# Two gate blocks ahead of the sets, single form loads in the weights' queue, single branch pieces, later gates' operands fetched at once

## The chip, the cores and the metric

The kernel runs on one core of a Trainium2 chip. Its engines each run their own instructions in order: TensorE (PE in the profile) multiplies matrices, VectorE (DVE) and ScalarE (ACT) work on tiles, GpSimd (POOL) and SyncE (SP) mainly start DMAs here. They wait for each other through semaphores. The metric is the device time of one execution in microseconds (us), the median of several runs.

## The reference

One decoder layer on 256 rows of width 2048, in float32:

```python
h = _rmsnorm(x, pre_norm_g)
proj = jnp.einsum('bsd,de->bse', h, w_in)
(q_a, c_kv, k_rope, z_mla, c_in, b_gate, c_gate, z_conv, g_mla, g_conv) = jnp.split(proj, cuts, axis=-1)
...
attn = attn.reshape(b, s, MLA_WIDTH) * jax.nn.silu(z_mla)
y_mla = jnp.einsum('bse,ed->bsd', attn, w_o_mla)
u = c_gate * c_in
...
y_conv = jnp.einsum('bse,ed->bsd', b_gate * conv * jax.nn.silu(z_conv), w_o_conv)
merged = jax.nn.sigmoid(g_mla) * y_mla + jax.nn.sigmoid(g_conv) * y_conv
out = jnp.einsum('bsd,de->bse', merged, w_out)
x = x + _rmsnorm(out, post_norm_g)
```

`attn` is causal latent attention with 16 heads of width 128 (query and key/value projections of rank 512, rotary part of 64), and `conv` a causal convolution of three taps over `u`. Apart from the latent projections, the weights of each path are 2048 by 2048.

## The kernel before

Every float32 product is made of three matmuls: each operand is split into a high part (ACT, `whi`, `shi_*`, line 252) and the rest (DVE, `wlo`, `slo_*`, line 253), and high·high, high·low and low·high are summed in PSUM. All matmuls have line 88 in the profile. Weights come in **units** of 1 MB (128 rows of 2048 values) through `load_raw` (line 164, queue of SP) into three buffers `raw`; a unit is split in two halves into `whi` and `wlo`, five buffers each.

**Heads** (0 to about 604 us, lines 520 to 1029). After the latent projections a loop goes over the 16 heads. In each, `channels(h, i)` makes the conv channels and `gates_turn` the gates z, with attention between them. The results are stored in DRAM as `far_at` and `far_cv`. Sprinkled into the heads 1 to 7 is the generator `make_forms` (lines 829 to 880), three steps a head: it loads the transposed input `xf` in two chunks of two DMAs (line 835), scales it (840), makes sums and differences of its quarters (851), splits each into high and low (856, 858, 860) in a tile `form` with two buffers, and stores it to `far_form` (863, POOL's queue, kept in program order). There are seven forms, of 1 MB each.

**Sets** (about 604 to 966 us). Work stands in a list `seq` of items `[load, split, mm, after]`. The driver (lines 1341 to 1368) issues at item j the loads of up to four later items that have one, then the splits of items up to j + 2, then item j's matmuls, then its `after`. Kinds of items:

- Plain units of `gate_block`, `branch_block` and `merged_block`: one weight unit, 24 matmuls. Four make a block of 512 output columns, and `last` treats the PSUM of the block: a gate block makes the sigmoid of `x @ W` and stores it (`keep`), a branch block multiplies by a gate fetched from DRAM (`again`) and stores, a merged block takes the second branch, multiplies, adds the first, turns the sum (line 330) and stores it to `far_m`.
- `paired(c)` for c = 1, 2, 3, the **sets** `s1` to `s3`: the columns of block c of both gates, computed by a scheme of Strassen's kind with seven products of half size in place of eight. The seven, in order `Q1 V5 V6 V7 V4 V3 Q2`, have two items each of 12 matmuls against a form (`sX`, `sY`, `sZ` in the profile). Their weights `b` (line 1174, SP's queue) lie in six buffers; `V5`, `V6` and `V4` add two weight tiles on DVE (line 1182), and `V5` starts a DMA of POOL that adds another tile in place (line 1186).
- `turned_unit`: loads stored pieces of `far_at` or `far_cv` into a `raw` buffer (line 1081) and splits them into `at_both` or `cv_both` (`split_turned`), with no matmul. `at_both` lies where `x_both`, the input of the gate blocks, lay.

`interleave(s, {...})` puts the listed plain and turned items between the items of the set's seven products. The order before: gate block 0 of the first gate (four units), then `s1` with the second gate's block 0 (`g0`), the pieces of `at_both` and the first branch blocks `p`, then `s2`, `s3`, then the merged blocks `v[2]`, `v[3]`. All seven forms are loaded back from `far_form` by POOL ahead of the list (line 1033).

In `merged_block`, `soon` runs after the second unit and fetches operands; for c = 2 and 3 it fetches for both row halves, and for c = 3 it also multiplies (line 1146) `m` (the first branch) by its gate `q`.

**Out stage** (about 966 us to the end, lines 1370 to 1479). `out_order` lists the 16 units of the last product: the first three K quarters of columns 0 and 1 (six units), their last quarters, then columns 2 and 3. `m_both[3]`, the last quarter of its input, comes from `far_m[3]` through the turned unit `last_m`: `last_m[0]` loads it in the first unit, `last_m[1]` splits it. It is needed from the seventh unit. After three units the tiles of the pool `late` are released, and ACT issues the loads of `gb` and `xr` (lines 1399, 1400) into other tiles there.

Where an instruction is not kept in program order by `tc.keep_in_program_order`, the framework may place it elsewhere in its engine's order.

Of the kernel before, what the change touches and what calls it, by code (L numbers as in the profile page):

```python
# [11 lines left out]
F32 = mybir.dt.float32  # L12
F32R = mybir.dt.float32r
I32 = mybir.dt.int32
AF = mybir.ActivationFunctionType
ALU = mybir.AluOpType
PSUM = bass.MemoryType.PSUM

P = 128
S = 256  # L20
NT = S // P
# [61 lines left out]
def tile_layer(ctx: ExitStack, tc: tile.TileContext, xw, w0, xb, x, pos, pvec, post_g, wc, wz, wcv, wkr, wqk, wqr, wv, cwr, wsq, xf, out):  # L83
    nc = tc.nc
# [16 lines left out]
    dram = ctx.enter_context(tc.tile_pool(name="dram", bufs=1, space=bass.MemoryType.DRAM))  # L101
# [17 lines left out]
    for h in range(H):  # L119
        g, second = divmod(h, HG)  # L120
# [23 lines left out]
    out_order = [(c, k) for c in range(2) for k in range(3)] + [(0, 3), (1, 3)]  # L144
    out_order += [(c, k) for c in (2, 3) for k in range(4)]
    u_out = {ck: add(wsq[4, ck[0], ck[1]]) for ck in out_order}
# [71 lines left out]
    def take(i):  # L218
        ahead(i)
        return pieces(splits.pop(i))  # L220
# [93 lines left out]
    n = 2 * XW // S  # L314
# [207 lines left out]
    for i in range(KD // 2):  # L522
# [3 lines left out]
        w = take(u_qa[i])  # L526
# [3 lines left out]
    for i in range(4):  # L530
        w = take(u_ckv[i])
# [9 lines left out]
    w = splits.pop(u_kr)  # L541
# [153 lines left out]
    def values(h, pt):  # L695
# [24 lines left out]
    far_at, far_cv, far_m = (  # L720
        [dram.tile([P, NT * 512], F32, name=f"far_{n}{g}") for g in range(4)] for n in ("at", "cv", "m")
    )
# [101 lines left out]
    cv_w = bp.tile([P, NT, 512], F32, name="cv_w")  # L824
    KH = KD // 2
    FORMS = ("11", "5", "6", "7", "22", "3", "12")
    far_form = {n: dram.tile([P, KH * 2 * P], F32R, name=f"far_form{n}") for n in FORMS}

    def make_forms():

        kq = KH // 2
        for c in range(2):
            area = at_f[:, 8:, :].rearrange("p (i k) s -> p i k s", i=2)
            for i in range(2):
                nc.sync.dma_start(out=area[:, i], in_=xf[i][:, c * kq * S : (c + 1) * kq * S].rearrange("p (k s) -> p k s", k=kq))
            yield
            for i in range(2):
                for k in range(kq):
                    x = area[:, i, k, :]
                    nc.vector.scalar_tensor_tensor(  # L840
                        x, x, col("pre_g", KH * i + kq * c + k), r_x[:, :], op0=ALU.mult, op1=ALU.mult
                    )
                yield
            a11, a21 = area[:, 0, :, :P], area[:, 0, :, P:]
            a12, a22 = area[:, 1, :, :P], area[:, 1, :, P:]
            u, w, f7, f3 = (
                cv_f[:, 8 + 2 * i : 10 + 2 * i, :].rearrange("p a (b s) -> p (a b) s", b=2) for i in range(4)
            )

            def tt(o, a, b, op):  # L850
                nc.vector.tensor_tensor(o, a, b, op=op)

            def part(n, src, sign=1.0):
                f = early_pool.tile([P, kq, 2, P], F32R, name=f"form{n}_{c}", tag="form", bufs=2)
                hi, lo = f[:, :, 0, :], f[:, :, 1, :]
                nc.scalar.activation(hi, src, AF.Copy, scale=sign)
                if sign == 1.0:
                    nc.vector.tensor_tensor(lo, src, hi.bitcast(F32), op=ALU.subtract)
                else:
                    nc.vector.scalar_tensor_tensor(lo, src, sign, hi.bitcast(F32), op0=ALU.mult, op1=ALU.subtract)  # L860
                w = kq * 2 * P
                return lambda: tc.keep_in_program_order(
                    nc.gpsimd.dma_start(
                        out=far_form[n][:, c * w : (c + 1) * w], in_=f[:, :, :, :].rearrange("p k j c -> p (k j c)")
                    )
                )

            goes = []
            for n, src, sign, s in (
                ("11", a11, 1.0, None), ("22", a22, 1.0, None), ("12", a12, 1.0, None), ("5", u, 1.0, (u, a22, a21, ALU.subtract)),  # L870
                ("6", w, -1.0, (w, u, a11, ALU.add)), ("7", f7, 1.0, (f7, a11, a21, ALU.subtract)),
                ("3", f3, 1.0, (f3, w, a12, ALU.subtract)),
            ):
                if s:
                    tt(*s)
                go = part(n, src, sign)
                yield
                go()
        while True:
            yield  # L880
# [16 lines left out]
    for h in range(H):  # L897
        v, at = divmod(h, HV)
# [56 lines left out]
        if 0 < h < 8:  # L955
            next(form_steps)
        channels(h, 2)
        if 0 < h < 8:
            next(form_steps)
        if 0 < h < 8:  # L960
            next(form_steps)

        steps = [make(*i, *([at == 3] if i[0] == "a" else [])) for i in made[h]]
# [62 lines left out]
    def again(key, t):  # L1026
        tc.keep_in_program_order(nc.gpsimd.dma_start(out=t[:, :], in_=kept[key][:, :]))  # L1027
# [1 line left out]


    form = {n: forms.tile([P, KH, 2, P], F32R, name=f"form_{n}") for n in FORMS}
    for n in FORMS:
        nc.gpsimd.dma_start(out=form[n][:, :, :, :].rearrange("p k j c -> p (k j c)"), in_=far_form[n][:, :])


    seq = []
# [36 lines left out]
    def turned_unit(far, both, first, queue=nc.sync):  # L1073


        box = []

        def load():
            t = wpool.tile([P, UNIT], F32, name=f"turned{len(seq)}_{first}", tag="raw", bufs=3)
            for i, f in enumerate(far):  # L1080
                queue.dma_start(out=t[:, i * 1024 : (i + 1) * 1024], in_=f[:, :])
            box.append(t)

        def split():
            for i in range(len(far)):
                for t in range(NT):
                    o = i * 1024 + t * 512
                    split_turned(box[0][:, o : o + 512], both[first + i], t)

        return [load, split, None, None]  # L1090
# [18 lines left out]
    def branch_block(c, both):  # L1109
# [19 lines left out]

        return block(c, 2, lambda k: both[k // 4][:, k % 4, :], {}, last)  # L1130

    def merged_block(c, both):

        got = []

        def fetch(t):
            g, m = (
                wide(f"v{n}{c}_{t}", "y", 2) if c < 2 else late.tile([P, 512], F32, name=f"v{n}{c}_{t}")
                for n in "gm"
            )  # L1140
            again(("gc", c, t), g)
            again(("y" if c == 3 else "m", c, t), m)
            if c == 3:
                q = late.tile([P, 512], F32, name=f"vq{t}")
                again(("gm", c, t), q)
                nc.vector.tensor_tensor(m[:, :], m[:, :], q[:, :], op=ALU.mult)  # L1146
            got.append((g, m))

        def soon():
            for t in range(1 if c < 2 else NT):  # L1150
                fetch(t)

        def last(pss):
            for t in range(NT):
                if len(got) <= t:
                    fetch(t)
                g, m = got[t]
                nc.vector.tensor_tensor(g[:, :], pss[t][:, :], g[:, :], op=ALU.mult)
                nc.vector.tensor_tensor(m[:, :], m[:, :], g[:, :], op=ALU.add)  # L1159
                go, _ = turned(m[:, :], g[:, :], 4, far_m[c][:, 512 * t : 512 * (t + 1)])  # L1160
                go()

        return block(c, 3, lambda k: both[k // 4][:, k % 4, :], {1: soon}, last)
# [100 lines left out]
    def interleave(s, after):  # L1264

        for name in ("Q1", "V5", "V6", "V7", "V4", "V3", "Q2"):
            seq.extend(s[name])
            seq.extend(after.get(name, []))
# [9 lines left out]
    class Late(list):  # L1278
# [10 lines left out]
    make_identity(nc, ident[:, :])  # L1289
    seq.extend(gate_block(0, 0, "gm", {}))  # L1290
    at_b, cv_b = Late("at"), Late("cv")
    at_u = [turned_unit(far_at[2 * i : 2 * i + 2], at_b, 2 * i) for i in range(2)]
    cv_u = [turned_unit(far_cv[2 * i : 2 * i + 2], cv_b, 2 * i) for i in range(2)]
    g0 = gate_block(0, 1, "gc", {})
    p = [branch_block(c, at_b) for c in range(4)]
    v = [merged_block(c, cv_b) for c in range(4)]
    s1, s2, s3 = (paired(c) for c in (1, 2, 3))
    gate_last, branch_last = s2["Q2"][1][3], p[2][3][3]
    p[2][3][3] = None
    s2["Q2"][1][3] = lambda: (gate_last(), branch_last())  # L1300
    interleave(s1, {
        "Q1": g0[:1], "V5": g0[1:2], "V6": g0[2:3], "V7": g0[3:] + at_u[:1], "V4": at_u[1:] + p[0][:2],
        "V3": p[0][2:], "Q2": p[1][:3],
    })
    interleave(s2, {
        "Q1": p[1][3:], "V5": p[2][:1], "V6": p[2][1:2], "V7": p[2][2:3], "V4": p[2][3:], "Q2": p[3][:1],
    })
    interleave(s3, {
        "Q1": p[3][1:2], "V5": p[3][2:3], "V6": p[3][3:] + cv_u[:1], "V7": cv_u[1:] + v[0][:1], "V4": v[0][1:3],
        "V3": v[0][3:], "Q2": v[1],  # L1310
    })
    m_b = Late("m")
    m_pool, late, lstack = {}, None, ExitStack()
# [65 lines left out]
    def out_products(pss, w, kk):  # L1379
        for t in range(NT):  # L1380
            out_product(pss[t], t, w, kk)

    pss = [[bank(f"out{c}_{t}") for t in range(NT)] for c in range(2)]
    for i, (c, kk) in enumerate(out_order[:3]):
        w = take(u_out[c, kk])
        if i == 0:
            last_m[0]()
        if i == 2:
            last_m[1]()
        out_products(pss[c], w, kk)  # L1390
    lstack.close()
    main.close()
# [65 lines left out]
        normed(t, 1536, 2048, rr)  # L1458
        store(t, 1536, 2048, og[:, t, cs])

    for c, kk in out_order[3:6]:
        out_products(pss[c], take(u_out[c, kk]), kk)
    for c in range(3):
        if c == 2:
            pss.append([bank(f"out{c}_{t}") for t in range(NT)])
# [105 lines left out]
```

## Time and profile before

| what | value |
| --- | --- |
| median of 3 runs | 1075.21 us (1072.54 to 1075.4) |
| the profiled execution | 1075.93 us |
| its span in the trace | 1074.1 us |
| DVE busy | 786.3 us (73%) |
| ACT busy | 577.5 us (54%) |
| POOL busy | 205.4 us (19%) |
| HBM traffic | 239.78 MB read, 28.31 MB written |

The span runs from the first to the last recorded instruction of the profiled execution. A name such as `out<-whi,m_both` gives the tile written and the tiles read. A row of the timeline has its start, its length, the engine, the source line, the operation and shape, the count, and in brackets the idle time ahead of it with the tile or instruction that ended it; `SPq`, `ACTq` and `POOLq` rows are what an engine's queue does by itself, such as starting DMAs. The granted clock is the share of full speed that TensorE's throttle granted.

### The profile page before, as it was taken

The page shows a single profiled execution, that of the slowest core. Times are in us where ns is not written, and L with a number is a line of the kernel's source. Part 1 is how long each engine was busy: PE and PEld are TensorE (multiplying, and loading weights), DVE is VectorE, ACT ScalarE, POOL GpSimd, SP SyncE. Part 2 cuts the span into 40 slices and gives each one's busy share as a digit, 9 for nine tenths or more (in the row PEclk, how much of TensorE's full clock was granted, in tenths as well). Part 3 has the DMA queues.
Part 4 walks back from the last instruction along what each step waited for, and adds up shares of the span by engine and source line. Part 5 has one row for each costly group of instructions (what it writes and reads, how often), then busy time and mean ns, then how long its engine had stood idle before and what let it go on. Part 6 is the DMA issues. An engine that isn't in the chain of part 4 may idle for free. (4 is left out here: it accounts for less than half of the span.)

```text
span 1074.1 us, 12900 instructions
## 1 busy us (share of the span) xinstructions
PE 1032.0 (96%) x4576; PEld 850.0 (79%) x4576; DVE 786.3 (73%) x1074; ACT 577.5 (54%) x811; POOL 205.4 (19%) x373
## 2 busy tenths in 40 slices
PE   9999999999899999999999979899999999997897
PEld 7877888888788888888888857688888788885686
DVE  7589778778587686877767738867889987554562
ACT  6764655645456465564654425655566665331551
POOL 4530311123311223112333201000101002241000
PEclk9998999999999999999999989999999999998899
DMA  9774768668788576756777799786877856777652
GB/s 366 275 256 161 284 217 279 241 208 297 252 281 276 186 282 234 247 207 204 283 243 248 253 396 342 304 342 208 242 287 253 283 194 225 247 273 291 231 191 79
DMA packets 55152, 273.12 MB, mean 254 GB/s; under 512 B 9232, under 2 KB 11920, under 8 KB 30512
## 3 DMA queue, kind: packets, MB, share of 16 engines
q1 hardware_dynamic: 34272, 205.96, 53.7%
q0 software_dynamic: 17792, 58.32, 17.2%
q10 hardware_dynamic: 3024, 8.01, 1.9%
q8 instruction: 36, 0.59, 0.2%
q14 instruction: 28, 0.23, 0.1%
HBM read 239.78 MB, written 28.31 MB: 250 GB/s over the span
## 5 line engine op out<-in xcount | busy, mean ns | idle before, releaser
L253 DVE TENSOR_TENSOR wlo<-raw,whi 128x1024 fp32r<-128x1024 f32 (+1 forms) x316 | 371.7, 1189 | 133.6 <-ACT whi L252 125.6
L252 ACT ACTIVATE whi<-raw 128x1024 fp32r<-128x1024 f32 (+1 forms) x318 | 323.7, 1030 | 268.3 <-PE cv L88 108.1
L88 PE MATMUL cv<-whi,x_both 128*128 128x512 f32 x1024 | 321.1, 390 | 0.1
L88 PEld LDWEIGHTS cv<-whi,x_both 128*128 128x128 f32 x1024 | 193.0, 188 | 40.6 <-DVE vv_lo L253 0.9
L88 PE MATMUL cv<-wlo,x_both 128*128 128x512 f32 x512 | 200.3, 391 | 0.1
L88 PEld LDWEIGHTS cv<-wlo,x_both 128*128 128x128 f32 x512 | 96.4, 188 | 20.5 <-DVE wlo L253 1.1
L252 ACT ACTIVATE shi_V<-b 128x1024 fp32r<-128x1024 f32 x60 | 62.1, 1056 | 50.0 <-DVE b L1182 24.4
L253 DVE TENSOR_TENSOR slo_V<-b,shi_V 128x1024 fp32r<-128x1024 f32 x60 | 71.3, 1219 | 18.8 <-ACT shi_V L252 18.1
L88 PE MATMUL z<-whi,x_both 128*128 128x512 f32 x256 | 80.3, 390 | 0.8 <-DVE at_f L406 0.8
L88 PE MATMUL sq<-whi,at_both 128*128 128x512 f32 x256 | 80.8, 389 | 0.0
L88 PE MATMUL sq<-whi,cv_both 128*128 128x512 f32 x256 | 79.5, 389 | 0.0
L88 PE MATMUL out<-whi,m_both 128*128 128x512 f32 x208 | 69.7, 414 | 6.2 <-ACT whi L252 6.2
L338 POOL DMA_DIRECT2D far<-via x64 | 35.3, 558 | 183.6 <-DVE via L330 182.5
L88 PEld LDWEIGHTS z<-whi,x_both 128*128 128x128 f32 x256 | 48.1, 188 | 11.1 <-DVE at_f L406 1.2
L88 PEld LDWEIGHTS sq<-whi,at_both 128*128 128x128 f32 x256 | 48.0, 188 | 10.0
L88 PEld LDWEIGHTS sq<-whi,cv_both 128*128 128x128 f32 x256 | 48.1, 188 | 9.9
L88 PEld LDWEIGHTS out<-whi,m_both 128*128 128x128 f32 x208 | 41.8, 201 | 16.1 <-ACT whi L252 7.0
L88 PE MATMUL sq<-wlo,at_both 128*128 128x512 f32 x128 | 49.9, 390 | 0.4 <-DVE wlo L253 0.4
L253 DVE TENSOR_TENSOR slo_Q<-b,shi_Q 128x1024 fp32r<-128x1024 f32 x24 | 29.2, 1224 | 28.6 <-ACT shi_Q L252 27.3
L88 PE MATMUL z<-wlo,x_both 128*128 128x512 f32 x128 | 49.8, 389 | 0.0
L88 PE MATMUL sq<-wlo,cv_both 128*128 128x512 f32 x128 | 49.8, 389 | 0.0
L88 PE MATMUL sX<-shi_V,form 128*128 128x512 f32 x144 | 47.0, 397 | 1.6 <-ACT shi_V L252 1.6
(282 smaller groups left out, 1608.5 us busy)
## 6 DMA issues: line engine op xcount, KB each, us to landing
raw<-wcv_dram SPq DMA_DIRECT2D x64, 1024.0 KB, 5.8
raw<-wsq_dram SPq DMA_DIRECT2D x56, 1024.0 KB, 6.2
b<-wsq_dram SPq DMA_DIRECT2D x24, 1024.0 KB, 5.9
raw<-wz_dram SPq DMA_DIRECT2D x16, 1024.0 KB, 5.3
raw<-wqk_dram SPq DMA_DIRECT2D x8, 1024.0 KB, 7.0
far_form<-form POOLq DMA_DIRECT2D x14, 512.0 KB, 7.2
form<-far_form POOLq DMA_DIRECT2D x7, 1024.0 KB, 23.0
cw<-cwr_dram POOLq DMA_DIRECT2D x24, 256.0 KB, 5.9
```

What stands on the lines that cost most here:

```text
L88: return tc.keep_in_program_order(nc.tensor.matmul(*a, **kw))
L252: a = nc.scalar.activation(hi, src, AF.Copy)
L253: b = nc.vector.tensor_tensor(lo, src, hi.bitcast(F32), op=ALU.subtract)
L338: tc.keep_in_program_order(queue.dma_start(out=f[i], in_=m))
```

## The change

- The steps of `make_forms` run in heads 0 to 7 (two in head 0, three after). Its `xf` loads are kept in program order, and one more `yield` stands between them and the scaling. `far_form` is declared F32, with bitcasts.
- The forms are no longer loaded by POOL in one go; `bring_form(n)` loads one on SP's queue, attached by `with_form` behind the load of a given item: two in the second gate block, four in set 1, one at the first unit of `p[1]`.
- The second gate's block 0 (`g0`) stands whole behind the first gate's, ahead of set 1.
- `at_u` and `cv_u` are four items of one piece each, where they were two items of two, and the branch and merged units are spread anew over the sets.
- The merged block c = 2 fetches all operands of c = 2 and 3 in its `soon`, and the product of `m` and `q` moves into `last`.
- `last_m[1]` runs in the fifth unit of the out stage instead of the third.

```diff
@@ make_forms
-                nc.sync.dma_start(out=area[:, i], in_=xf[i][...])
+                tc.keep_in_program_order(
+                    nc.sync.dma_start(out=area[:, i], in_=xf[i][...])
+                )
+            yield
             yield
@@ head loop
         channels(h, 2)
-        if 0 < h < 8:
+        if h < 8:
             next(form_steps)
-        if 0 < h < 8:
             next(form_steps)
@@ forms
-    for n in FORMS:
-        nc.gpsimd.dma_start(out=form[n][...], in_=far_form[n][:, :])
+    def bring_form(n):
+        nc.sync.dma_start(
+            out=form[n][:, :, :, :].rearrange("p k j c -> p (k j c)").bitcast(F32), in_=far_form[n][:, :]
+        )
@@ merged_block
+            q = None
             if c == 3:
                 q = late.tile([P, 512], F32, name=f"vq{t}")
                 again(("gm", c, t), q)
-                nc.vector.tensor_tensor(m[:, :], m[:, :], q[:, :], op=ALU.mult)
-            got.append((g, m))
+            got.append((g, m, q))
 
         def soon():
-            for t in range(1 if c < 2 else NT):
-                fetch(t)
+            if c < 2:
+                fetch(0)
+            elif c == 2:
+                for f in fetches[2:]:
+                    for t in range(NT):
+                        f(t)
@@ last
-                g, m = got[t]
+                g, m, q = got[t]
+                if q:
+                    nc.vector.tensor_tensor(m[:, :], m[:, :], q[:, :], op=ALU.mult)
@@ the list
-    at_u = [turned_unit(far_at[2 * i : 2 * i + 2], at_b, 2 * i) for i in range(2)]
-    cv_u = [turned_unit(far_cv[2 * i : 2 * i + 2], cv_b, 2 * i) for i in range(2)]
+    at_u = [turned_unit(far_at[i : i + 1], at_b, i) for i in range(4)]
+    cv_u = [turned_unit(far_cv[i : i + 1], cv_b, i) for i in range(4)]
...
+    seq.extend(g0)
+    def with_form(u, n):
+        old = u[0]
+        u[0] = lambda: (old(), bring_form(n))
+    with_form(seq[4], "11")
+    with_form(seq[6], "5")
+    for name, n in (("Q1", "6"), ("V5", "7"), ("V6", "22"), ("V4", "3")):
+        with_form(s1[name][1], n)
+    with_form(p[1][0], "12")
     interleave(s1, {
-        "Q1": g0[:1], "V5": g0[1:2], "V6": g0[2:3], "V7": g0[3:] + at_u[:1], "V4": at_u[1:] + p[0][:2],
-        "V3": p[0][2:], "Q2": p[1][:3],
+        "Q1": at_u[:1] + p[0][:1], "V5": at_u[1:2] + p[0][1:2], "V6": at_u[2:3] + p[0][2:3], "V7": at_u[3:] + p[0][3:],
+        "V4": p[1][:2], "V3": p[1][2:3], "Q2": p[1][3:],
     })
     interleave(s2, {
-        "Q1": p[1][3:], "V5": p[2][:1], "V6": p[2][1:2], "V7": p[2][2:3], "V4": p[2][3:], "Q2": p[3][:1],
+        "Q1": p[2][:1], "V5": p[2][1:2], "V6": p[2][2:3], "V7": p[2][3:], "V4": p[3][:2], "Q2": p[3][2:3],
     })
     interleave(s3, {
-        "Q1": p[3][1:2], "V5": p[3][2:3], "V6": p[3][3:] + cv_u[:1], "V7": cv_u[1:] + v[0][:1], "V4": v[0][1:3],
-        "V3": v[0][3:], "Q2": v[1],
+        "Q1": p[3][3:] + cv_u[:1], "V5": cv_u[1:2] + v[0][:1], "V6": cv_u[2:3] + v[0][1:2], "V7": cv_u[3:] + v[0][2:3],
+        "V4": v[0][3:] + v[1][:1], "V3": v[1][1:2], "Q2": v[1][2:],
     })
@@ out stage, the first three units
-        if i == 2:
-            last_m[1]()
@@ the next three
-    for c, kk in out_order[3:6]:
-        out_products(pss[c], take(u_out[c, kk]), kk)
+    for i, (c, kk) in enumerate(out_order[3:6]):
+        w = take(u_out[c, kk])
+        if i == 1:
+            last_m[1]()
+        out_products(pss[c], w, kk)
```

More of the change, by code (lines that the diff above doesn't have):

```diff
@@ L826, in tile_layer @@
     FORMS = ("11", "5", "6", "7", "22", "3", "12")
-    far_form = {n: dram.tile([P, KH * 2 * P], F32R, name=f"far_form{n}") for n in FORMS}
+    far_form = {n: dram.tile([P, KH * 2 * P], F32, name=f"far_form{n}") for n in FORMS}
     def make_forms():
@@ L834, in make_forms @@
             for i in range(2):
-                nc.sync.dma_start(out=area[:, i], in_=xf[i][:, c * kq * S : (c + 1) * kq * S].rearrange("p (k s) -> p k s", k=kq))
+                tc.keep_in_program_order(
+                    nc.sync.dma_start(out=area[:, i], in_=xf[i][:, c * kq * S : (c + 1) * kq * S].rearrange("p (k s) -> p k s", k=kq))
+                )
+            yield
             yield
@@ L863, in part @@
                     nc.gpsimd.dma_start(
-                        out=far_form[n][:, c * w : (c + 1) * w], in_=f[:, :, :, :].rearrange("p k j c -> p (k j c)")
+                        out=far_form[n][:, c * w : (c + 1) * w], in_=f[:, :, :, :].rearrange("p k j c -> p (k j c)").bitcast(F32)
                     )
@@ L1031, in tile_layer @@
     form = {n: forms.tile([P, KH, 2, P], F32R, name=f"form_{n}") for n in FORMS}
-    for n in FORMS:
-        nc.gpsimd.dma_start(out=form[n][:, :, :, :].rearrange("p k j c -> p (k j c)"), in_=far_form[n][:, :])
+    def bring_form(n):
+        nc.sync.dma_start(
+            out=form[n][:, :, :, :].rearrange("p k j c -> p (k j c)").bitcast(F32), in_=far_form[n][:, :]
+        )
     seq = []
@@ L1130, in branch_block @@
         return block(c, 2, lambda k: both[k // 4][:, k % 4, :], {}, last)
+    fetches = []
     def merged_block(c, both):
@@ L1145, in fetch @@
                 again(("gm", c, t), q)
-                nc.vector.tensor_tensor(m[:, :], m[:, :], q[:, :], op=ALU.mult)
-            got.append((g, m))
+            got.append((g, m, q))
         def soon():
-            for t in range(1 if c < 2 else NT):
-                fetch(t)
+            if c < 2:
[4 more added lines that the diff above has]
+                        f(t)
+        fetches.append(fetch)
         def last(pss):
```

## The prediction

> **What bounds the kernel now.** I read the page's head and busy shares first.
>
> ```profile
> span 1074.1 us, 12900 instructions
> ...
> PE 1032.0 (96%) x4576; PEld 850.0 (79%) x4576; DVE 786.3 (73%) x1074; ACT 577.5 (54%) x811; POOL 205.4 (19%) x373
> ```
>
> TensorE (PE) is busy for 1032.0 of 1074.1 us. The change alters no matmul, so what it can win is PE's 42.1 us of idleness and whatever PE runs at a lowered clock. The second view, PE's waits by releaser, says where the idleness is.
>
> ```profile
> PE sX L88 <- ACT shi_Q L252: 6.3, 1, 6.3
> PE out L88 <- ACT whi L252: 6.2, 2, 3.7
> PE out L88 <- DVE wlo L253: 4.0, 3, 2.7
> PE kn L88 <- DVE at_f L742: 3.6, 2, 3.1
> PE sc L88 <- DVE kn L253: 3.5, 1, 3.5
> PE sX L88 <- DVE slo_V L253: 3.5, 2, 2.2
> ```
>
> The columns are total, times and longest. Six lines hold 27.1 us. `sX` belongs to the sets (604 to 966 us), `out` to the last stage, `kn`, `sc` to the heads. The third view, windows, prices them with the clock (columns: PE, weight loads, DVE, ACT, POOL with counts; granted clock; DMA share; GB/s).
>
> ```profile
> 616.00:660.00 44.00, 34.32 (x128) 26.33 (x127) 22.35 (x17) 15.69 (x17) 7.02 (x12) 0.84 1.02 390
> 660.00:700.00 40.00, 34.94 (x146) 27.90 (x145) 33.15 (x32) 26.14 (x33) 0.00 (x0) 0.96 0.87 304
> 700.00:800.00 100.00, 100.00 (x443) 82.81 (x442) 78.64 (x65) 57.21 (x59) 5.09 (x8) 1.00 0.76 262
> 800.00:850.00 50.00, 48.26 (x212) 39.28 (x211) 46.37 (x41) 33.77 (x39) 3.98 (x6) 1.00 0.77 251
> 950.00:1005.00 55.00, 44.84 (x167) 34.96 (x166) 27.70 (x32) 15.65 (x18) 13.12 (x24) 0.88 0.78 286
> 82.20:89.10 6.90, 6.16 (x21) 5.39 (x22) 6.90 (x12) 2.33 (x5) 0.00 (x0) 0.51 0.80 251
> 20.00:100.00 80.00, 75.59 (x328) 62.20 (x327) 60.50 (x106) 47.66 (x76) 29.55 (x49) 0.96 0.70 245
> 628.30:638.70 10.40, 5.85 (x13) 4.13 (x13) 3.41 (x3) 4.72 (x6) 0.00 (x0) 0.51 1.04 418
> 976.50:980.00 3.50, 3.50 (x10) 2.69 (x9) 0.15 (x1) 0.00 (x0) 1.98 (x4) 0.51 0.78 208
> ```
>
> An undisturbed stretch makes 443 matmuls in 100 us, 0.2257 us each; a unit of 24 takes 5.4 us, one of 12 takes 2.7. Against that pace the windows lose (length / 0.2257 − count) × 0.2257: **15.1 us** in 616–660, **7.0** in 660–700, **2.1** in 800–850, **17.3** in 950–1005. That is more than the waits, since after an idle stretch PE ran at a clock of 0.51: for 3.5 us from 976.5, for most of 628.3–638.7. In 20–100 PE idles 4.4 us and loses 3.4 more to the clock of 82.2–89.1 (6.9 × 0.49). These places are the terms of the sum.
>
> **The change part by part.** *Start of the sets.* Before, one gate block ends at 626.1 and the first set's `Q1` follows; its weights and all seven forms are requested together.
>
> ```profile
> 616.71 5.93 SPq L1174 DMA_DIRECT2D b<-wsq_dram  x6
> ...
> 631.28 2.00 ACT L252 ACTIVATE shi_Q<-b 128x1024 fp32r<-128x1024 f32 x2 [7.14 <-DMA b<-wsq_dram]
> ...
> form<-far_form POOLq DMA_DIRECT2D x7, 1024.0 KB, 23.0
> b<-wsq_dram SPq DMA_DIRECT2D x6, 1024.0 KB, 24.8
> ```
>
> The last two rows are the DMA view of 616–665 (count, size, median us to landing). Thirteen 1 MB loads start within 6 us; at the 390 GB/s of the window 1 MB takes 2.7 us, so they fill 35 us. `Q1`'s first `b` lands only at 631.28. The change puts the second gate block first: four units × 5.44 = 21.8 us of PE work that needs neither forms nor sets. `Q1` then starts near 648, when half of the burst is in. The 6.3 us wait and its slow clock go. But those four units' weights, and then the first `turned` piece and branch unit, share the same bandwidth: if the six `b` and the forms still leave when their buffers come free, the branch weights needed near 651 are requested around 627–632 behind the backlog, and land at 653–661. That is a stall of 2–10 us and some 2–3 us of low clock. The lower bound of the loss is 0 (the new form order spreads the burst), the upper 15, as much as now. I take 9 left, nearer to the upper row, as six `b` for 35 us ahead were issued in 5.9 us here. **Gain 6** (0 to 15).
>
> The form loads move from seven POOL issues to seven SP issues, under 1 us each on SP by the `b` row (5.93 for six), beside transfers of 2.7 us each: nothing, unless one waits at SP's head for its buffer, which is free for all seven from the start. The row 616–660 says what counts: a DMA share of 1.02 at 390 GB/s with two issuing engines. The Trainium skill ("DMA: Bandwidth & Descriptors", section "Issuing engines are not separate DMA queues") states that transfers started by different engines run on the same 16 DMA engines and interleave. The trace agrees with its 1.02; by that rule the move of queue alone would leave all 15 us. It is the first rival below.
>
> *V4 stall of set 1.*
>
> ```profile
> 684.61 0.39 PE L88 MATMUL sq<-whi,x_both 128*128 128x512 f32 x1
> ...
> 680.83 4.49 DVE L1182 TENSOR_TENSOR b<-b,b 128x2048 f32<-128x2048 f32 x2
> 685.23 2.35 DVE L253 TENSOR_TENSOR slo_V<-b,shi_V 128x1024 fp32r<-128x1024 f32 x2
> 687.50 4.90 DVE L253 TENSOR_TENSOR at_both<-turned,at_both 128x512 fp32r<-128x512 f32 x8
> 692.32 2.35 DVE L253 TENSOR_TENSOR slo_V<-b,shi_V 128x1024 fp32r<-128x1024 f32 x2
> ```
>
> The eight `at_both` subtractions (4.90 us) run in one row between two `slo_V` splits that PE waits for, because `at_both` lies over the tile that the second gate block reads until 684.6 (`x_both`, first row). With that block ended before the set and each piece (1.2 us of DVE) alone in its group, they no longer queue. What is late next is DVE in a `V5` or `V6` group: two adds 4.49, two splits 4.7, one piece 1.2, one branch split 2.35, 12.7 us against PE's 10.9. With splits two units ahead, one or two such groups in a row cost up to 1.8 us each in sets 1 and 3. I leave 1.5. **Gain 5.5** (3 to 7). The 2.1 us of 800–850, the same stall of set 3 with `cv_both`, halve: **gain 1** (0 to 2).
>
> *Out stage.* In 950–1005 one chain runs from DMA to DMA.
>
> ```profile
> 967.41 0.69 DVE L1158 TENSOR_TENSOR vg<-sq,vg 128x512 f32<-128x512 f32 x1 [2.02 <-DMA vg<-kept_gc]
> 971.30 0.69 DVE L1146 TENSOR_TENSOR vm<-vm,vq 128x512 f32<-128x512 f32 x1 [0.60 <-DMA vq<-kept_gm]
> 974.11 4.38 POOL L338 DMA_DIRECT2D far_m<-vg  x8 [7.33 <-DVE vg L330]
> 983.08 0.34 ACTq L1399 DMA_DIRECT2D gb<-post_g_dram  x1
> 983.50 11.58 DMA turned<-far_m
> 995.11 1.15 ACT L252 ACTIVATE m_both<-turned 128x512 fp32r<-128x512 f32 x2 [9.07 <-DMA turned<-far_m]
> ```
>
> The last merged block's PSUM is ready by 965.7, as DVE waits for the DMA of `vg` alone until 967.4, and `vq` lands only at 971.3, the stores start at 974.1, `gb` (whose buffer the stores free) goes at 983.1 and blocks ACT's next weight split until then; `m_both` waits until 995.1 ahead of the fourth unit's split. Fetching the operands a block earlier leaves DVE with two each of 0.69 (multiply), 0.69, 0.65, 0.67: 5.4 us, so stores start near 971 and `gb` and `turned` go 3 us earlier. Ten more POOL issues a block earlier cost 5.5 us of POOL, idle then (share 19%); what they could delay is POOL's own `turned` load of the block before, by at most 5.5 us, needed two units later. The wait for `turned` moves two units (10.9 us) back, so it lands near 992, 26 us into the stage, while the sixth unit, whose split is queued on ACT behind it, begins at 27: with 3.4 us of splits that is 1.5–2.5 us late, plus 1.7 of clock. Bounds: 0 left, or 10 left (`gb` still holds ACT and the sixth unit runs late). I leave 4. **Gain 13.3** (7 to 17).
>
> *Head.*
>
> ```profile
> 76.30 1.67 DVE L840 SCALAR_TENSOR_TENSOR at_f<-at_f,pv,r_x 128x256 f32<-128x256 f32 x4 [2.29 <-DMA at_f<-xf_dram]
> 276.03 0.63 ACT L856 ACTIVATE form<-at_f 128x512 fp32r<-128x512 f32 x1 [9.11 <-DMA far_form<-form]
> SPq L835 <- DVE cv_f L851: 9.8, 1, 9.8
> ```
>
> The form work waits 2.29 us in DVE's order for `xf`, right ahead of the `at_f` that `kn` waits for (3.6 us), and near 276 ACT waits 9.11 us for a form store, ahead of the `sc` stall (3.5). The pinned load with one more turn between it and its first use takes away the first wait; the second is another buffer's. The same instructions remain, so DVE's 76% of 20–100 stays. Best: the 7.8 us of 20–100 and the 3.5 of `sc`, 11, less what other stalls there keep; worst: a new stall of the same size. **Gain 4** (−5 to 10).
>
> Sum: 6 + 5.5 + 1 + 13.3 + 4 = 29.8. The profiled execution took 1075.93 (span 1074.1 and 1.8 around it), 0.7 above the median of 1075.21: 1075.9 − 29.8 = **1046**, by the median 1045.4.
>
> **The rivals.** *A, the burst stays:* the loads leave when buffers come free, whatever their queue; the start then keeps 13–15 us, the out stage keeps up to 7, the head gives nothing. For: 1.02 and six `b` in 5.9 us. Against: 21.8 us more cover. Gain 1 + 5 + 1 + 10 + 0 = 17 or a little more: 1055–1060. *B, every hole closes:* 15.1 + 7.0 + 2.1 + 17.3 = 41.5: 1034. For: DVE 73% and ACT 54% have room. Against: groups of 12.7 us on DVE and the late `turned`. *C, nothing comes of it:* what one place gives is waited for at the next, since DMA runs at 0.76–0.87 after 660: 1073–1078. *D, slower:* the pinned `xf` load sits at the head of SP's queue, with the weight loads behind it, until `cv_f` frees its area (the 9.8 us row). Three `raw` buffers of 5.4 us cover 16 us; a hold of 16 + x stalls PE by x. Four pinned loads would have to cost over 30 us together, each above 7.5 past its cover; at 10 each it is 41, so 1087. Against: the loads after the first of each pair find their area free.
>
> **How the numbers follow.** Forecast 1040–1051: 0.46. A (1052–1066): 0.25. B (1031–1039): 0.17, and 0.02 below. C: 0.05. D: 0.05. The range 1033–1066 leaves out C, D and the low end of B, some 0.16. About 0.3% (3.2 us) is what a measurement of this kernel can tell from no change: faster 0.90, same 0.05, slower 0.05.
>
> **What would show it.** Right: `sX <- ACT shi_Q` is gone from PE's waits; 604–648 runs at full clock; any stall of the first set names a branch split released by a `raw` landing; no `at_both` row of eight; `out <- ACT whi` falls from 6.2 to below 3. Wrong: DMA share below 0.9 in 620–650 with no stall behind it (B); a hole above 8 us near 651 (A); SP waiting over 16 us at L835 with `whi` late in the heads (D).

## The result and the profile after

| | before | after |
| --- | --- | --- |
| median | 1075.31 us (4 runs, 1072.54 to 1077.29) | 1062.72 us (4 runs, 1059.47 to 1064.04) |
| profiled execution, span | 1075.93, 1074.1 us | 1064.04, 1062.3 us |
| first matmul of the gate block | 604.16 us | 598.04 us |
| first matmul of `out` | 961.57 us | 959.71 us |
| end of the last matmul of `out` | 1066.34 us | 1054.21 us |

The kernel became faster by 12.6 us: the ratio is 0.988, its 95% interval 0.9847 to 0.9913. The forecast was 1046, with 1033 to 1066 as the range. By the marks in the table (read from PE's timeline) the head became 6.1 us shorter, the stage of the sets **4.3 us longer** (357.4 to 361.7), and the out stage 10.3 us shorter (104.8 to 94.5). The forecast had −4, −12.5 (6, 5.5 and 1) and −13.3. So the sets are what failed.

PE's waits by releaser after the change (total, times, longest):

```profile
PE sq L88 <- ACT whi L252: 20.4, 1, 20.4
PE out L88 <- DVE wlo L253: 3.9, 2, 3.1
...
PE sc L88 <- DVE kn L253: 2.0, 1, 2.0
PE out L88 <- ACT whi L252: 1.0, 1, 1.0
```

The `shi_Q` wait of 6.3 us has shrunk to 0.7, the `slo_V` and `shi_V` waits are gone, and those of `out` fell from 10.2 to 4.9. One new wait of 20.4 us outweighs what the sets won. The windows of the changed kernel, in the columns of before, give its place and its price with the clock:

```profile
604.00:650.00 46.00, 43.92 (x191) 35.30 (x189) 22.90 (x20) 16.85 (x18) 5.84 (x10) 1.00 0.98 378
650.00:700.00 50.00, 29.14 (x115) 23.39 (x115) 30.07 (x28) 22.88 (x27) 1.99 (x3) 0.76 0.75 260
700.00:800.00 100.00, 100.00 (x443) 82.84 (x442) 86.36 (x71) 63.14 (x65) 5.14 (x8) 1.00 0.76 264
800.00:850.00 50.00, 49.76 (x219) 40.59 (x218) 44.94 (x42) 34.32 (x41) 4.04 (x6) 1.00 0.83 274
950.00:1005.00 55.00, 50.15 (x212) 40.53 (x211) 31.63 (x33) 22.67 (x26) 9.46 (x18) 0.97 0.83 316
```

At the pace of 0.2257 us a matmul, 650–700 loses (221.5 − 115) × 0.2257 = **24.0 us**, of which 20.4 are the one wait and most of the other 3.6 the low clock that follows it (0.53 in 668–678); 800–850 loses 0.6 instead of 2.1, 950–1005 loses 7.2 instead of 17.3.

The wait is that of the first branch unit, `p[0][0]`, the first item with matmuls behind `Q1`. SP's timeline shows its request, and the timelines of ACT and PE what came of it:

```profile
622.35 0.33 SPq L1036 DMA_DIRECT2D form<-far_form  x1
625.38 2.76 SPq L1189 DMA_DIRECT2D b<-wsq_dram  x2
632.76 0.33 SPq L1036 DMA_DIRECT2D form<-far_form  x1
633.19 0.41 SPq L1086 DMA_DIRECT2D turned<-far_at  x1
635.51 3.06 SPq L1036 DMA_DIRECT2D form<-far_form  x2
641.04 0.33 SPq L164 DMA_DIRECT2D raw<-wsq_dram  x1
```

```profile
630.30 0.33 ACTq L1026 DMA_DIRECT2D kept_gm<-sg  x1
630.74 2.96 ACT L252 ACTIVATE whi<-raw 128x1024 fp32r<-128x1024 f32 x3 [9.05 <-DMA b<-wsq_dram]
...
669.42 2.00 ACT L252 ACTIVATE whi<-raw 128x1024 fp32r<-128x1024 f32 x2 [13.05 <-DMA raw<-wsq_dram]
```

```profile
670.53 0.80 PE L88 MATMUL sq<-whi,at_both 128*128 128x512 f32 x1 [20.39 <-ACT whi L252]
```

The weight is requested at 641.04, lands at 669.3 and is split at 669.42; PE had been ready for it since 650.1. Ahead of it in SP's queue stand the six `b` of `Q1`, `V5` and `V6` and all seven forms. Only `Q1`'s two `b` and form 11 among these are used before it. When it is requested, 5.5 MB of these loads and of `turned` have not landed yet.

What moved until it landed shows in the DMA view of 641.04 to 669.34 (packets, MB, share of the engines' time):

```profile
q1 hardware_dynamic: 1069, 6.74, 57.5%
q0 software_dynamic: 448, 2.62, 40.1%
```

By the sizes, `q1` is SP's queue and `q0` POOL's; ACT's moved another 0.52 MB. POOL requested its two loads that add into the `b` of `V5` at 642.58 and 651.83, after the branch weight, and two fetches of `y` from 652.4; all four landed before it. They moved 2.62 MB in 40.1% of 28.3 us, 11.3 us, or 4.3 us per MB; SP's 6.74 MB took 2.4 us per MB. It isn't POOL's queue that is slow: in e2 below, where POOL brings the forms, 6.91 MB of plain loads took 46.9% of 35.7 us (616.05 to 651.74), 2.4 us per MB. So it is most likely the adding that costs; no run here leaves it out.

### The profile page after: what moved, and what is told of

Its sections match the earlier page's. It is cut to its first block, busy times and chain, and to the rows that moved or that the text cites. A ratio compares the mean times of both kernels' runs of the same rounds, so it can differ in the third digit from the quotient of the medians.

```text
span 1062.3 us, 12896 instructions
## 1 busy us (share of the span) xinstructions
PE 1020.0 (96%) x4576; PEld 843.5 (79%) x4576; DVE 785.3 (74%) x1074; ACT 580.4 (55%) x811; POOL 200.7 (19%) x366
## 4 chain that ended last, share of the span: by engine, by line
PE 70%; DMA 15%; DVE 8%; issue 4%; ACT 2%; POOL 1%; DVEq 0%; ACTq 0%; POOLq 0%; SPq 0%
PE cv L88 25%; PE sq L88 15%; PE out L88 6%; DMA raw<-wsq_dram 4%; PE z L88 4%; PE sX L88 4%; DMA form<-far_form 3%; DMA far_form<-form 3%; PE sZ L88 3%; DVE wlo L253 2%; PE qa L88 2%; PE ckv L88 2%; DMA cw<-cwr_dram 2%; PE kn L88 2%; PE qn L88 2%
## 5 line engine op out<-in xcount | busy, mean ns | idle before, releaser
L88 PE MATMUL sq<-whi,at_both 128*128 128x512 f32 x256 | 83.3, 398 | 20.4 <-ACT whi L252 20.4
L253 DVE TENSOR_TENSOR slo_V<-b,shi_V 128x1024 fp32r<-128x1024 f32 x60 | 71.8, 1222 | 21.0 <-ACT shi_V L252 20.1
L88 PE MATMUL out<-whi,m_both 128*128 128x512 f32 x208 | 66.0, 396 | 1.0 <-ACT whi L252 1.0
L88 PE MATMUL z<-wlo,x_both 128*128 128x512 f32 x128 | 49.8, 389 | 0.0
L88 PE MATMUL out<-wlo,m_both 128*128 128x512 f32 x104 | 41.3, 397 | 3.9 <-DVE wlo L253 3.9
```

The costliest lines, as they stand in the source:

```text
L88: return tc.keep_in_program_order(nc.tensor.matmul(*a, **kw))
L253: b = nc.vector.tensor_tensor(lo, src, hi.bitcast(F32), op=ALU.subtract)
```

## The experiments

Two theories of the hole were set against each other, and later two more. **Q**: the branch weight stands behind loads that are not needed yet. **V**: the first set needs more bytes than DMA brings, whatever their order. **S**: SP has too many loads to issue. **H**: SP's own waiting at each issue makes the request late. Times are medians; ratios are against the kernel before. "Request" and "landing" are the times from the start of the gate block to the request and the landing of the first branch weight; PE is ready for it 49 to 53 us after that start (650.1 − 598.0 in the changed kernel). "Sets" is the time from that start to the first matmul of `out`, 357.4 us in the kernel before.

| kernel | us | ratio (95%) | request | landing | hole at the first branch unit | sets |
| --- | --- | --- | --- | --- | --- | --- |
| changed | 1062.72 | 0.988 (0.9847–0.9913) | 43.0 | 71.3 | 20.4 | 361.7 |
| e1 forms in place | 1054.66 | 0.9823 (0.9789–0.9856) | 38.1 | 66.4 | 16.7 | 356.1 |
| e2 forms by POOL | 1062.66 | 0.9894 (0.9866–0.9922) | 38.1 | 71.5 | 19.6 | 362.4 |
| e11 set weights in place | 1054.24 | 0.9832 (0.9784–0.988) | 35.2 | 49.8 | 2.7 | 352.0 |
| e4 both in place | 1051.55 | 0.9794 (0.976–0.9828) | 28.4 | 38.9 | 0.3 | 352.2 |

**e1: the forms kept at their places.**

```diff
     def bring_form(n):
-        nc.sync.dma_start(out=form[n]..., in_=far_form[n][:, :])
+        tc.keep_in_program_order(nc.sync.dma_start(out=form[n]..., in_=far_form[n][:, :]))
```

> The changed kernel, with each form's load kept at its place in SP's queue: forms 3 and 12 then stand behind the first branch units' weights instead of ahead of them. Theory Q (the 20.4 us hole at 650 is the first branch weight standing in one queue behind loads that are not needed yet): two forms of 1 MB fewer ahead at 2.6 us each, and as much less waiting at the queue's head, so the hole shrinks by 5 to 10 us to 10 to 15, and the kernel takes 1052 to 1058. Rival V (the first set needs more bytes than the DMA engines can bring, in whatever order): the hole moves or splits, the same 20 us in sum, 1060 to 1064.

The time fell as Q said, to 1054.66, but the hole only to 16.7, just above its 10 to 15. The request came 5 us earlier after the gate block's start (38.1 instead of 43.0) and still took 28.3 us to land: 5.5 MB (three `b` of `V5` and `V6`, forms 7 and 22, half a MB of `turned`) were under way, and POOL's loads again took 40% of the DMA time until then. The stage of the sets became 5.6 us shorter. The rest of the 8 us lies elsewhere: this execution's head was 2.7 us shorter, and its out stage had no hole at the fifth unit.

**e2: the forms by POOL in one go.**

```diff
     def bring_form(n):
-        nc.sync.dma_start(
+        nc.gpsimd.dma_start(
...
+    for n in FORMS:
+        bring_form(n)
...
-    with_form(seq[4], "11")
...
-    with_form(p[1][0], "12")
```

> The changed kernel, with all seven forms loaded by POOL in one go ahead of the sets, as before the change; nothing else is undone. Theory Q: as many bytes go out ahead of the first branch weight as in the changed kernel, so the queue that starts them matters little: a hole of 12 to 20 us near 650, 1055 to 1063. Rival S (SP's issuing is what is late: seven loads fewer in its queue let the branch weight go by 634 instead of 641): hole below 10, 1050 to 1054. If sharing the engines slows the second gate block's own weights, that block shows stalls before 648 instead.

1062.66, the time of the changed kernel, as Q said, with a hole of 19.6 and the landing at 71.5 instead of 71.3. The request went 4.9 us earlier, and the load then took 33.4 us. Which engine starts the form loads makes no difference to the time that these runs show; rival S, the issuing, falls.

**e11: the sets' weights kept at their places, the forms left free.**

```diff
-                nc.sync.dma_start(out=t[:, :], in_=wsq[n, c, k])
+                tc.keep_in_program_order(nc.sync.dma_start(out=t[:, :], in_=wsq[n, c, k]))
```

> The changed kernel with the sets' own weights kept at their places in SP's queue and the forms left to the framework, which puts five of them ahead of the first branch weight and the weights of V5 and V6 behind it. Theory Q in bytes: ahead of the first branch weight stand, from the second gate block's third unit on, about 10.5 MB instead of 14; at 2.6 us each it lands 8 to 10 us earlier than in the changed kernel, so the hole at 650 shrinks to 8 to 13 us and the time is 1050 to 1056. Rival H (what matters is that SP waits for a landing before each issue, and the forms stand there): the hole stays at 16 to 20 us, 1058 to 1063.

SP's timeline of this kernel:

```profile
619.22 8.86 SPq L1036 DMA_DIRECT2D form<-far_form  x5
632.70 0.32 SPq L1086 DMA_DIRECT2D turned<-far_at  x1
635.49 0.33 SPq L164 DMA_DIRECT2D raw<-wsq_dram  x1
635.92 0.38 SPq L1189 DMA_DIRECT2D b<-wsq_dram  x1
```

Five forms still go ahead of the branch weight, with SP waiting among them (8.86 us for five), yet the weight requested at 635.49 lands at 650.08, 14.6 us later instead of 28.3, and the hole is 2.7. The DMA view of these 14.6 us has nothing from POOL, only SP's queue and 0.45 MB of ACT's:

```profile
q1 hardware_dynamic: 854, 5.68, 92.6%
```

H's hole of 16 to 20 did not come, so the forms at which SP waits do not make it by themselves. Waiting still has a part: of the 21.5 us by which the landing came earlier, 7.8 are an earlier request. Q's bytes were counted too low: with the weights of `V5` and `V6`, POOL's accumulating loads into them (2 MB) and two `y` fetches, which wait for those weights or for POOL, also move behind the branch weight. The five forms still stood ahead, so the four `b` with what hangs on them were the larger part of the hole. How much of it is the four `b` and how much POOL's loads alone, no run separated; by the two DMA views POOL's took 11.3 of the 28.3 us.

**e4: forms and sets' weights in place** (the edits of e1 and e11 together).

> As the first, and the sets' own weight loads are kept at their places too, so SP's queue holds the loads in the order of their use. Theory Q: ahead of the first branch weight stand 3.5 MB of the sets' and forms' loads instead of 10, it lands by 645, the hole at 650 is below 3 us, and the kernel takes 1042 to 1048, unless a load that waits for a buffer at the queue's head now holds later ones (then a hole of up to 6 us in V5 to V7, 1048 to 1053). Rival V: 1060 to 1064 with the stalls spread over Q1 to V4.

1051.55 us, the lowest median here, 11 us below the changed one; the hole is gone. From e11 it cannot be told apart: the intervals overlap, and the stage of the sets is as long (352.2 and 352.0). With the `b` in place, the place of the forms is worth nothing that these runs show. The time missed Q's 1042 to 1048 and lies in the range that it gave for a new hold in `V5` to `V7`. The windows of ten us show why, of the changed kernel:

```profile
628.00:638.00 10.00, 9.37 (x41) 7.43 (x40) 5.60 (x5) 5.68 (x6) 0.00 (x0) 1.00 1.01 426
638.00:648.00 10.00, 9.27 (x40) 7.13 (x38) 4.25 (x4) 2.68 (x4) 0.96 (x1) 1.00 1.03 405
648.00:658.00 10.00, 1.43 (x5) 0.86 (x5) 4.25 (x4) 1.75 (x3) 1.99 (x3) 0.78 1.02 311
658.00:668.00 10.00, 0.00 (x0) 0.00 (x0) 0.00 (x0) 0.00 (x0) 0.00 (x0) 0.50 1.02 341
668.00:678.00 10.00, 7.00 (x17) 5.18 (x18) 7.49 (x7) 5.89 (x7) 0.00 (x0) 0.53 0.48 185
678.00:688.00 10.00, 10.00 (x46) 8.27 (x45) 9.95 (x9) 7.32 (x8) 0.00 (x0) 1.00 0.44 152
```

and of e4:

```profile
631.00:641.00 10.00, 10.00 (x46) 8.29 (x45) 4.24 (x4) 4.25 (x4) 0.00 (x0) 1.00 1.01 423
641.00:651.00 10.00, 9.70 (x43) 7.76 (x42) 6.86 (x7) 7.81 (x11) 0.71 (x1) 1.00 0.98 389
651.00:661.00 10.00, 9.33 (x41) 7.34 (x41) 8.87 (x9) 4.61 (x6) 2.25 (x4) 1.00 1.03 313
661.00:671.00 10.00, 8.77 (x39) 6.93 (x38) 10.00 (x8) 4.43 (x5) 0.00 (x0) 1.00 1.00 290
671.00:681.00 10.00, 6.73 (x24) 4.83 (x23) 5.59 (x7) 5.37 (x7) 0.00 (x0) 0.83 0.81 312
...
651.00:711.00 60.00, 51.87 (x201) 39.80 (x201) 46.70 (x41) 30.07 (x35) 3.35 (x6) 0.91 0.83 289
```

The DMA column stays at 1.0 for 40 us and more in both. In the changed kernel it falls to 0.48 and 0.44 as soon as PE has its weight: much of what the next units need had come ahead of it. In e4 PE works on what has come, with waits of 0.7 to 2.8 us between 659 and 706. But 651–711 still loses (265.8 − 201) × 0.2257 = 14.6 us there, with POOL's adding loads under way from 650.3 to 670.7, against the 24.0 us that 650–700 lost in the changed kernel. So V is right in part: the order won 9.4 us of the 24.0. What holds PE in the rest is mixed. The longest wait, 2.8 us at 677.9, is for a weight that took 23.7 us to land; in 661–671 DVE was busy without a break.

**e3: the sets as before, head and out stage as changed.** Undone are the order of the sets, the single pieces and the single form loads:

```diff
-    seq.extend(g0)
...
     interleave(s1, {
-        "Q1": at_u[:1] + p[0][:1], ...
+        "Q1": g0[:1], "V5": g0[1:2], "V6": g0[2:3], "V7": g0[3:] + at_u[:1], ...
```

> The changed kernel with the sets' order, the pieces in pairs and the forms by POOL in one go as before the change; the head and the merged blocks with the out stage stay changed. If the three parts add up as the traces' marks say (head 6.1 us won, sets 4.3 lost, out stage 10.3 won): 1057 to 1061, faster than the changed kernel, with PE waiting again for shi_Q by about 6 us and at V4. If the stages depend on each other (what the head wins is waited for at the sets' first loads): 1064 to 1070.

1059.36 us (ratio 0.986, 0.9826 to 0.9894): as the sum of the marks said. The sets' part of the change, as it was made, cost about 3 us, though the intervals of the two kernels overlap. PE again waits 5.9 us for `shi_Q`, and 5.9 and 2.3 in V4, where it waited 5.1 before the change. The 8.2 stand in e5 and e10 too and the 5.1 in e6: the changed head costs 3 us there, and why was not tried.

**e10: e3 with the loads in the order of use** (the edits of e1 and e11 on e3, forms attached along set 1).

> The third experiment (sets in the order of before, pieces in pairs, head and out stage changed) with forms on SP's queue and the sets' weights and forms kept in the order of their use. If putting both gate blocks first has a worth of its own (21.8 us of cover for Q1's weights and the first forms): PE still waits 4 to 8 us for the first shi_Q near 620 and at V4, 1054 to 1060, slower than the fourth experiment by 3 us or more. If the order of the loads is all that counts: 1048 to 1053, as the fourth.

1054.2 us (0.9813, 0.9778 to 0.9848), at the edge of both expectations. Its waits:

```profile
PE sX L88 <- ACT shi_V L252: 5.9, 1, 5.9
...
PE sX L88 <- DVE slo_V L253: 2.7, 2, 2.3
PE sX L88 <- ACT shi_Q L252: 2.4, 1, 2.4
PE sX L88 <- ACT sg L1107: 2.2, 1, 2.2
```

The `shi_Q` wait fell from 5.9 to 2.4, but 2.2 us for `sg`, at 622.5, stand ahead of the same product, so `Q1` still waits 4.6; V4's 8.2 us stayed. These are the waits of the first expectation. The time is 5.2 us below e3 and 2.7 above e4, with intervals that overlap in both cases; the stage of the sets is 355.0 us, against 352.2 in e4. So by the marks the order of the loads and the new order of the units both gain, the second some 3 us, and the times are too close to confirm either here.

**e5 and e6: the head alone, and the merged blocks with the out stage alone, on the kernel before** (their hunks of the diff above; the forms stay with POOL).

> The kernel before with the head's part of the change alone (the form steps from head 0, the xf loads kept in program order, one more turn). If the head's gain stands by itself: the gate block starts 5 to 7 us earlier, and the time is 1067 to 1071. If the sets' first loads then wait as much longer (they go out when the head's tiles are released, so nothing should hold them): 1073 to 1076.

> The kernel before with the edits of the merged blocks and the out stage alone (operands fetched a block earlier, the product with q in the last step, the split of m_both two units later). If the out stage's gain stands by itself: 1062 to 1067, with PE's waits for out down from 10 to 3 to 5 us. If head and out together give less than the sum of the two alone, the two runs differ from the run of both by over 3 us.

The head alone gave 1070.92 us (0.9969, 0.995 to 0.9987), a gain of some 3 us; the out stage alone 1062.38 (0.9892, 0.9863 to 0.9921), some 11. Their sum, 14, is close to e3's 15. PE's waits for `out` fell in e6 to one, 3.14 us.

**e7 and e8: the out stage taken apart**, both on the changed kernel.

```diff
# e7
+        if i == 2:
+            last_m[1]()
...
-        if i == 1:
-            last_m[1]()
...
# e8
-            if c < 2:
-                fetch(0)
-            elif c == 2:
-                for f in fetches[2:]:
...
+            for t in range(1 if c < 2 else NT):
+                fetch(t)
```

> The changed kernel with the split of m_both[3] back in the third unit of the out stage. Theory M (the moved wait is what the out stage gains by: the far_m piece lands 24 to 27 us into the stage, and the fourth unit's split, queued behind it on ACT, begins at 16): PE waits 5 to 8 us more near the fourth unit, 1067 to 1072. Rival F (the earlier fetch does it, and the piece now lands early enough): at most 1.5 us more, 1062 to 1064.

> The changed kernel with each merged block fetching its own operands again; the product with q stays in the last step and the split in the fifth unit. Theory F: the last block's chain starts 3 to 5 us later, so the store, gb and the far_m piece come as much later, and ACT's split behind gb is late: 3 to 6 us more, 1065 to 1069. Theory M: the piece has 6 us to spare in the fifth unit, and 0 to 2 us are lost, 1062 to 1065.

e7 took 1062.24 us (0.9896, 0.9879 to 0.9914), no loss: theory M falls. e8 took 1069.66 (0.9969, 0.9948 to 0.999), 7 us lost, a little more than F said. The two ACT timelines show both at once, that of the changed kernel:

```profile
972.44 0.34 ACTq L1423 DMA_DIRECT2D gb<-post_g_dram  x1
...
974.63 2.01 ACT L252 ACTIVATE whi<-raw 128x1024 fp32r<-128x1024 f32 x2 [0.97 <-DMA raw<-wsq_dram]
984.77 1.16 ACT L252 ACTIVATE m_both<-turned 128x512 fp32r<-128x512 f32 x2 [8.12 <-DMA turned<-far_m]
986.51 2.01 ACT L252 ACTIVATE whi<-raw 128x1024 fp32r<-128x1024 f32 x2 [0.58 <-DMA raw<-wsq_dram]
```

and that of e8:

```profile
980.96 0.34 ACTq L1419 DMA_DIRECT2D gb<-post_g_dram  x1
...
981.90 2.01 ACT L252 ACTIVATE whi<-raw 128x1024 fp32r<-128x1024 f32 x2 [14.61 <-issue]
993.44 1.15 ACT L252 ACTIVATE m_both<-turned 128x512 fp32r<-128x512 f32 x2 [9.53 <-DMA turned<-far_m]
994.50 3.89 ACT L252 ACTIVATE whi<-raw 128x1024 fp32r<-128x1024 f32 x4
```

In e8, as before the change, `m_both` stands between the fourth and the fifth unit's split, although the source calls it in the fifth unit; it does so in the changed kernel and in e7 too. The framework had chosen this place from the start, so moving the call moved nothing. What helped is that `gb` goes at 972.4 instead of 981.0, which is 12.7 us after the first matmul of `out` instead of 20.1. POOL's timeline of e8 shows why the late fetch costs so much:

```profile
960.76 0.57 POOL L1086 DMA_DIRECT2D turned<-far_m  x1 [6.36 <-ACT whi L252]
961.32 0.57 POOL L1029 DMA_DIRECT2D vg<-kept_gc  x1
...
971.84 4.38 POOL L338 DMA_DIRECT2D far_m<-vg  x8 [7.26 <-DVE vg L330]
```

The fetches stand behind the block's own `turned` load, which waits 6.4 us in POOL's order. Fetched a block earlier, they are ahead of it.

## Why the prediction was wrong

**Start of the sets: the step that failed.** The mechanism was named, "the branch weights needed near 651 are requested around 627–632 behind the backlog, and land at 653–661", with "9 left" and a gain of 6. In the run the weight was requested at 641.04 and landed at 669.34. With V4's stall the text left 10.5 us of loss at the start of the sets; 604–650 lost 2.9 and 650–700 lost 24.0. Two steps were wrong.

- The request. With three buffers in turn, the weight's was free at about 633, when DVE ended the first of three `wlo` that began at 631.83. That was late already: ACT had stood idle for 9.05 us until 630.74, behind a store (`kept_gm`) that was issued only when a `b` had landed. SP then held the request for 8 us more behind two forms, each of which went when a `b` had landed.
- The time to land. The text priced 1 MB at 2.7 us in one backlog of loads of SP and forms. The sum had no term for POOL's two adding loads, which the kernel before has too; with the `y` fetches they took 11.3 of the 28.3 us here.

The price of 9 came from the row of six `b` issued in 5.9 us, which shows only that loads go early, not what is then late. Gain 6 became a loss. The sign that the text set for rival A, "a hole above 8 us near 651", came; A's own price (13 to 15 left) was too low as well, and its 1055 to 1060 just missed the 1062.72. That lies in the 1052 to 1066 that had A's chance, but with a larger loss in the sets than A's, and more won in the head than A gave.

**The first cover was right:** with 21.8 us more before `Q1` its wait fell from 6.3 to 0.7, and 604–648 ran at full clock. **V4's stall** went as forecast, but probably in part by luck: no stall of PE over 0.5 us remains between 680 and 850, and the hole ahead gave the loads and DVE 20 us to catch up. In e11 and e4, where the hole is 2.7 and 0.3, PE waits 4.9 and 3.5 us for `slo_V` and `shi_V` in set 1, more than the 1.5 us left for `V5` and `V6`. **800–850** gained 1.5 for a forecast of 1.

**The queue of the forms:** counted at nothing, and e2 confirms it (1062.66 against 1062.72). What the move from POOL to SP did not do is put them in order; the text's lower bound was that "the new form order spreads the burst", and e1 shows that this needed them to be kept in place.

**Out stage:** −10.3 for a forecast of −13.3, by the right step (the earlier fetch, 7 us in e8) and a wrong one. The move of the wait for `turned` by two units did not happen (e7), and so "the sixth unit" was the fifth. The text had also misread the rows before: the `m_both` of 995.11 stands behind the fourth unit's split, that of 984.03, and ahead of the fifth's. And of the ten POOL issues that it moved a block ahead, four stood there before. The rest of the miss is a hole of 3.1 us in the first unit that was not in the sum: its `wlo` stands on DVE behind the last block's chain, which runs until 962.

**Head:** forecast −4, −6.1 by the marks of one execution and about −3 by the times of e5. All lie within the range given, but one mark says little: over the ten profiled executions with the changed head the gate block begins between 593.1 and 603.9, at 598.4 in the mean, and over the two with the old head at 604.2 and 602.1. Which of its edits does it was not tried apart.

**Rivals C and D** did not come: PE's waits after the change hold no stall in the heads above 2.3 us. In D's sum, four loads at 10 us are 40, not 41. Within the sets, though, something like C did happen: what `Q1` won was waited for, and more, at the next item.

## What to carry to other kernels

Where the DMA engines are busy all the time, count the bytes that are under way when a load is issued and those that other queues issue before it lands, and compare its landing with the moment of its use. A load that goes as soon as its buffer is free can cost time, because it stands in front of others. When a change spaces loads out in the source, look in the trace whether they really go in that order, and keep them there if the framework is free to move them. The same holds for waits: a call that is moved in the source may stand where it stood.

## What the runs showed of the hardware

A load's time to land followed the DMA time of everything that moved meanwhile: one and the same 1 MB load took 28.3 us in the changed kernel, in which 9.9 MB moved, and 14.6 in e11, in which 6.2 MB moved, with the DMA column at 1.0 in both. POOL's adding loads (with the small `y` fetches) took 4.3 us per MB, plain loads 2.4 on SP's queue as on POOL's.

And SP's issues waited for landings of loads with which they share no data. Of the changed kernel, SP's waits from 605 to 660:

```profile
SPq L1036 <- DMA form<-far_form: 6.6, 2, 4.5
SPq L1036 <- DMA b<-wsq_dram: 4.3, 2, 2.4
SPq L1189 <- DMA raw<-wsq_dram: 2.7, 1, 2.7
SPq L164 <- DMA form<-far_form: 2.4, 1, 2.4
```

A form load has no use for a `b`, nor a `raw` load for a form; still each went just after one had landed, up to 4.5 us late. The chain of work that ended last shows the pattern (start, length):

```profile
611.15 11.18 DMA form<-far_form
...
622.35 18.62 DMA form<-far_form
...
641.04 28.30 DMA raw<-wsq_dram
```

The form of 622.35 goes when that of 611.15 has landed, and the branch weight, which is the eighth DMA issued by SP and ACT after it, goes when that form has landed. In the changed kernel eleven issues between 619 and 646 went within 0.1 us of a landing, two of them stores of ACT, which held up its splits; each has in the trace the same completion semaphore as the DMA whose landing it followed. And in each of the twelve traces at most eight DMAs of SP and ACT together are under way at once. So the eight look like semaphores that the compiled program uses in turn; every run has eight, so what the limit costs was not measured.

The length of the head, which differed by up to 11 us between profiled executions with the same head, stays unexplained.
